# Dense operands on multiples of 512 bytes, early state-space inputs, and seven PSUM banks for the dense products of a two-block model

## The chip, the core and the metric

The kernel runs on one core of one Trainium2 chip. The metric is the device time of one execution in microseconds, less is better. A profile is one execution on the chip, taken by the hardware profiler; its times are counted from the first instruction. Engines are called PE (matrix products), DVE (vector), ACT (activations), POOL (the general engine) and SP (which issues the DMAs).

## The reference, cut to what matters

Two different transformer-like blocks run one after the other on x of 1024 tokens by 1024 channels, all in float32.

```
def reference(x, ...):
    x = first_block(x, ...)     # retention + sparse attention, then conv_ffn
    return second_block(x, ...) # rwkv7 time mix + S5 state space, then gated ffn

first_block:  proj = rmsnorm(x) @ w_in             # 1024 x 6424
              merged = sig(ga) * (retention @ w_ret_o) + sig(gb) * (nsa @ w_nsa_o)
              x = x + merged @ w_out
              x = x + (gelu(conv3(h @ w_up_a)) * (h @ w_up_b)) @ w_down   # 2816 wide
second_block: proj = modulate(rms_norm(x)) @ w_in  # 1024 x 2304
              mix = [rwkv7(z), s5_mix(u)] @ w_out ; x = x + g_m * mix
              x = x + g_f * ((silu(h @ gate) * (h @ up)) @ down)          # 2816 wide
```

`s5_mix` first turns its parameters (`s5_a_re`, `s5_a_im`, `s5_log_dt`, `s5_b`, `s5_c`) into tables: decay and rotation of each state, their powers, and products with b and c. The tables depend on the parameters alone.

## The kernel before, in words

**Dense products.** Activations lie transposed, channels on the 128 partitions and tokens along the row. One dense product (`proj`, with `mm3`, L204) takes 128 output channels by 512 tokens. Each weight block of 128 by 128 and each activation is split into a rounded high part and the rest (`whi`, `wlo`; for instance `fh`, `fl`), and three fp32r matmuls per block are summed: high by high, high by rest, rest by high. A product over 1024 channels is 24 matmuls; one of `ffn`'s down products over 5 or 4 blocks is 15 or 12. Every matmul streams 512 columns (2048 bytes per partition, the moving operand) past 128 columns of weights (512 bytes per partition). `mm3t` (L212) has it the other way round: activations are the stationary operand, and 256 columns of weights (`w2hi`, `w2lo`) are streamed; it is run for the retention's values (768 matmuls) and for `u_proj` (384).

**Weights.** `wload` (L180 to L183): SP loads 512 KB into `wraw` (two buffers, a third one in part of the kernel), ACT rounds it to `whi`, POOL subtracts to get `wlo`. `whi` and `wlo` have two buffers each.

**PSUM.** There are 8 banks of 128 by 512. `PM` (name `mm`) has 2, and every dense product takes one of them in turn; `PN` has 1. The other 5 are given to the stage that runs: in the second part the pools `mb0`, `mb1`, `mb2` of the class `Banks` with 2, 2 and 1 (`b`), which the two chains of the RWKV recurrence, its side work, and (through `any`) transposes and state-space work use. A bank is free again when ACT or DVE has copied its sum out: for the first half of an up product ACT copies to `at` (L1548), for the second DVE multiplies `ct` by it (L1572).

**Order.** Instructions are written in program order, and a scheduler that simulates the engines puts them into each engine's queue; queues run in order. The attention and the RWKV recurrence are small dependent steps. Dense products of other parts (`fill`) are placed between their steps by hand-written dependencies (`beside_attention`, `side_by_side`). The stages, in us: norm and projections to 170, attention with dense products beside it to 640, retention to 940, merge and output of block one to 1170, ffn of block one for the first 512 tokens with the state-space tables (`s5_prep`) step by step beside it to 1600, projections of block two to 1756, state space and recurrence for either half with dense products beside them to 3053, the rest dense to the end.

**State-space tables.** `s5_prep` (L954) is a generator; its first step loads `s5_a` to `s_araw` (L966, L967) and `s5_log_dt` to `s_dt` with two DMAs of 1024 elements of 4 bytes (L976), transposes (L971), takes an exponential on ACT (L977) and runs some 55 small DVE instructions; its second step loads `s_B` (L1048). One step is written after each step of the ffn (`f10`), the first after the ffn's first.

**Addresses.** Tiles are put one after the other, pools stacked from both ends of a partition. Bytes past a multiple of 512 at which a row of an operand begins in the kernel before:

```
whi, wlo (all of wload but the state space's)     160
fh, fl (ffn, half a sequence), yr, yn (merge)     160
ah, al (ffn, hidden)                               96
hh, hl (block one's input), Mh, Ml, mo, mh, ml    480
zh and its own whi, wlo (state space)             480
w2hi, w2lo of the retention / of u_proj       0 / 480
```

All of them are multiples of 32. By the loops, 5,136 of the matmuls of L204 stream an operand at 160 (fh and fl, with wlo: 4,560; yr 384; yn 192), 2,112 one at 96, and 3,120 one at 480.

Of the kernel before, what the change touches and what calls it, by code (L numbers as in the profile page):

```python
# [85 lines left out]


CHUNK_DECAY = [float(np.exp(np.log1p(-np.exp2(np.float32(-5.0 - h))) * np.float32(128.0))) for h in range(4)]


class Banks:
# [12 lines left out]
    def any(self):  # L104
        self.n += 1
        return self.chain((0, 1, 0, 1, 2)[self.n % 5])


class Ctx:
    def __init__(self, tc, I, ctx):  # L110
        self.tc, self.nc, self.I, self.ctx = tc, tc.nc, I, ctx
        self.C = ctx.enter_context(self.pool("C", 1))
        self.PM = ctx.enter_context(self.pool("PM", 2, space=PSUM))
        self.PN = ctx.enter_context(self.pool("PN", 1, space=PSUM))
        self.DR = ctx.enter_context(self.pool("DR", 1, space=DRAM))
        self.ident = self.const("ident", self.C)
        self.ones = self.const("ones", self.C)
        self.W = None
        self.n_ins = 0
        self.WX = None  # L120
        self.n_w = 0

    def pool(self, name, bufs=1, side=None, space=None):
# [7 lines left out]
    def alloc(self, name, bufs=1, side=None):  # L131
        kw = {} if side is None else {"side": side}
        return self.tc.alloc_tile_pool(name=name, bufs=bufs, reuse_waits="tile", **kw)

    def const(self, name, pool):
# [79 lines left out]
    def proj(self, srcs, a, evac, kt=KT, nt=2, pool=None):  # L215
        w = self.wload(srcs, kt, pool)
        for t in range(nt):
            ps = self.PM.tile([128, 512], F32, name="mm")
            self.mm3(ps, w, a, t, kt)
            evac(t, ps)  # L220
# [142 lines left out]
class Nsa:  # L363
    def __init__(self, g, a, w_in, par, dst, dv, cx):
        self.g, self.a, self.w_in, self.par, self.dst, self.dv = g, a, w_in, par, dst, dv
        cp = cx.enter_context(g.pool("nc", 1))
        self.gate = cp.tile([128, 8, 24], F32, name="gate")
        self.kcd = [cp.tile([128, 2, 64], F32R, name=f"kcd{x}") for x in range(2)]
        self.vc4 = cp.tile([128, 2, 128], F32R, name="vc4")
        self.ap = cx.enter_context(g.pool("ac", 1))  # L370
        self.pq = cx.enter_context(g.pool("pq", 2, space=PSUM))
        self.pt = cx.enter_context(g.pool("pt", 2, space=PSUM))
        self.po = cx.enter_context(g.pool("po", 1, space=PSUM))
        self.tsel, self.tedge, self.tcmp = (g.const(n, self.ap) for n in ("tsel", "tedge", "tcmp"))
        self.valid, self.keep, self.force, self.nsl = (g.const(n, self.ap) for n in ("valid", "keep", "force", "nslope"))

# [46 lines left out]
    def compress(self, tp):  # L423

        g, nc, I, par = self.g, self.g.nc, self.g.I, self.par
        for kv, nm in ((0, "k"), (1, "v")):
            w1 = tp.tile([128, 16, 256], F32, name="cw1")
            w2 = tp.tile([128, 2, 64], F32, name="cw2")
            nc.sync.dma_start(w1, I["cmp_w1_" + nm][0].rearrange("(l p) n -> p l n", p=128))
# [8 lines left out]
            for j in range(2):  # L438
# [3 lines left out]
                nc.scalar.activation(hid[:, j], ps, AF.Gelu_apprx_tanh, bias=b1[:, j:j + 1], scale=1.0)  # L442
            c32 = tp.tile([64, 2, 64], F32, name="c32")
            nc.vector.memset(c32, 0.0)
# [273 lines left out]

def retention(g, a, w_in, gn_g, D_, yp, side_job, rest, early):


    with ExitStack() as cx:
        P = {n: cx.enter_context(g.pool("r" + n)) for n in ("tp", "vp")}
        P.update({n: cx.enter_context(g.pool("r" + n, b, space=PSUM)) for n, b in (("p1", 2), ("p2", 2), ("p3", 1))})
        sp = cx.enter_context(g.pool("rsj"))
        P.update({n: g.const(n, P["tp"]) for n in ("zeta", "xi")})
        for h in range(4):
            retention_head(g, a, w_in, gn_g, D_["gab"], D_["yr"], h, P, early)
            if h == 0:
                yn = load_split(g, yp, D_["yn"], 4, "yn")  # L730
            if h == 1:
                r = side_job(sp)
        rest()
    return r, yn
# [160 lines left out]
def nsa_phase(g, par, D_):  # L895
# [16 lines left out]
    with ExitStack() as cx:  # L912
        N = Nsa(g, a, w_in, par, D_["yn"], D_["nv"], cx)
        with g.pool("cp") as cp:
# [3 lines left out]
            N.compress(cp)  # L918
        N.tp = cx.enter_context(g.pool("at", 2))
        for gr in range(2):  # L920
            if gr:
# [31 lines left out]

def s5_prep(g, I, T, bank):  # L954

    nc, tc = g.nc, g.tc
    V, P = nc.vector, nc.gpsimd
    with ExitStack() as cx:
# [5 lines left out]

        are_im = tp.tile([32, 128], F32, name="s_araw")
        nc.sync.dma_start(are_im[0:16], I["s5_a_re_2"][0].rearrange("(a b) p -> a (b p)", b=2))  # L966
        nc.sync.dma_start(are_im[16:32], I["s5_a_im_2"][0].rearrange("(a b) p -> a (b p)", b=2))  # L967
        ps = bank()
# [4 lines left out]
        dt = small("dt")  # L973
        ld = I["s5_log_dt_2"]
        for b in range(2):
            nc.sync.dma_start(dt[b * 64:(b + 1) * 64], bass.AP(tensor=ld.tensor, offset=ld.offset + b, ap=[[0, 64], [2, 16]]))  # L976
        nc.scalar.activation(dt, dt, AF.Exp)  # L977
        x, mag, ang, n, r = (small(k) for k in ("x", "mag", "ang", "n", "r"))
# [529 lines left out]
class Ffn:  # L1508


    def __init__(self, g, D_, par):
        self.g, self.D, self.par = g, D_, par
        self.P = P = g.alloc("F")
        self.h = tuple([P.tile([128, 512], F32R, name=f"f{x}{k}") for k in range(KT)] for x in "hl")
        self.x = [P.tile([128, 512], F32, name=f"fx{k}") for k in range(KT)]
        self.carry = P.tile([128, NF, 2], F32, name="carry")
        self.r = {}
# [40 lines left out]
    def up(self, kind, hf, f, j, last):  # L1558
# [5 lines left out]
        else:  # L1564
            c = P.tile([128, 512], F32, name="ct", bufs=2)
            g.proj(I["ffn_w_gate_2"][0][:, f * 128:(f + 1) * 128], self.h, lambda t, ps: nc.scalar.activation(c, ps, AF.Silu), nt=1)
            w = I["ffn_w_up_2"][0][:, f * 128:(f + 1) * 128]
        hi = P.tile([128, 512], F32R, name=f"ah{j}")
        lo = P.tile([128, 512], F32R, name=f"al{j}")

# [103 lines left out]
class Mixer:  # L1674


    def __init__(self, g, D_, F, par, ad, banks):
        self.g, self.D, self.F, self.par, self.ad, self.banks = g, D_, F, par, ad, banks
        self.zc = F.P.tile([128, 14], F32, name="zc")
        self.s5c = F.P.tile([128, 2, 16], F32, name="s5c")  # L1680
        self.Sc = F.P.tile([128, 4, 2, 64], F32, name="Sc")

# [77 lines left out]
def second_part(g, D_, par, par2, ad, merged, dst):  # L1760
# [19 lines left out]
    def out2(hf):  # L1780
        acc = F.acc("nacc2")
        M.out(hf, acc)
        F.rstd_of(acc, (2, hf))

    acc = F.acc()
    take(out1(g, D_, m, 0, acc, F.P, banks.any, F.x))
# [8 lines left out]
    f10 = F.steps(1, 0)  # L1795
    prep = s5_prep(g, g.I, T, banks.any)
    for _ in range(54):
# [13 lines left out]
    M.z_proj(0, a, x3)  # L1811
    hp.release()
    M.mix(0, U, T)
    up.release()
# [19 lines left out]
    with g.pool("yo", side="right") as F.yo:  # L1834
# [3 lines left out]
        fill = g.products()  # L1838
        side_by_side(g.tc, M.groups, fill, PER_GROUP[1], LAG, SLACK, more=MORE[1])
        out2(1)  # L1840
        F.norm(2, 1)
# [6 lines left out]
    cx.close()  # L1848
    F.P.release()


# [36 lines left out]
def build(tc, I, dst):  # L1888
    with ExitStack() as ctx:
        g = Ctx(tc, I, ctx)  # L1890
        par, par2 = {}, {}
        D_ = {n: g.DR.tile([r, S], F32, name="d_" + n) for n, r in
              (("yn", 512), ("gab", 3 * D + 256 * EARLY), ("yr", D), ("x1", D), ("x3", D), ("x4", D), ("zd", 1792), ("mix", D))}
# [8 lines left out]
        g.W.release()  # L1902
        g.st.release()


# [26 lines left out]
```

## Time and profile before

| | us |
|---|---|
| median of 3 runs | 3532.59 (3530.93 to 3536.27) |
| profiled execution, its own time | 3534.38 |
| its span, first to last instruction | 3532.60 |
| PE busy | 3365.9 (95%) |
| DVE, ACT, POOL busy | 1717.1, 1333.5, 1456.5 |

Read it so: a matmul's record is longer than the time until the next matmul starts, because they are pipelined. Where matmuls follow each other without a gap, the time of one is the distance of starts, and the busy time of PE is their number by that distance. An idle time is told in brackets with what ended it.

### The profile page before, as it was taken

Reading aid. Unit: us, or ns where it says so; the run is one execution under the profiler, and the core shown is the slowest. Engines: PE = TensorE matmul, PEld = TensorE weight load, DVE = VectorE, ACT = ScalarE, POOL = GpSimd, SP = SyncE. Lnnn points to the kernel's source line nnn. Section 1 sums busy time; section 2 is a strip of 40 time slices with the busy share of each in tenths; the row PEclk is TensorE's granted clock in tenths of the full one; section 3 lists DMA queues with packets and bytes.
Section 4 is the critical chain, followed back from the end, with each engine's and each line's share of the span. In section 5 each row is a group of like instructions: output and inputs, shape, how many; then the busy total and the mean of one; then the engine's idle time right before and its main releaser. Section 6 shows DMA issues by size and latency. Waiting matters only on the chain. (4 is left out here: it accounts for less than half of the span.)

```text
span 3532.6 us, 49520 instructions
## 1 busy us (share of the span) xinstructions
PE 3365.9 (95%) x19080; PEld 2721.0 (77%) x19080; DVE 1717.1 (49%) x3317; ACT 1333.5 (38%) x2171; POOL 1456.5 (41%) x1089
## 2 busy tenths in 40 slices
PE   7999999999999798998989999999899999999998
PEld 6988788878788677877877777768777777778887
DVE  4456556465434665345575545565744344341112
ACT  4245346422333322343234434433353433342223
POOL 2333433210144344553555444324554443345544
PEclk9999999999999899999999999989999999999999
DMA  5211111455634334234533122134441222353332
GB/s 147 73 53 52 59 62 43 133 175 167 196 122 137 106 101 149 85 111 120 181 117 115 58 80 67 52 106 150 144 135 58 71 65 61 100 181 96 91 94 90
DMA packets 521845, 371.02 MB, mean 105 GB/s; under 512 B 33756, under 2 KB 457866, under 8 KB 520842
## 3 DMA queue, kind: packets, MB, share of 16 engines
q1 hardware_dynamic: 521610, 367.85, 34.2%
q8 instruction: 151, 2.47, 0.3%
q14 instruction: 84, 0.69, 0.1%
HBM read 313.43 MB, written 54.03 MB: 104 GB/s over the span
## 5 line engine op out<-in xcount | busy, mean ns | idle before, releaser
L183 POOL TENSOR_TENSOR wlo<-wraw,whi 128x1024 fp32r<-128x1024 f32 (+2 forms) x460 | 945.0, 2057 | 1301.7 <-PE mm L204 726.2
L182 ACT ACTIVATE whi<-wraw 128x1024 fp32r<-128x1024 f32 (+2 forms) x460 | 418.1, 909 | 762.0 <-PE mm L204 619.8
L204 PE MATMUL mm<-fh,whi 128*128 128x512 f32 x1520 | 621.2, 410 | 35.3 <-DVE ct L1572 17.8
L204 PE MATMUL mm<-fl,whi 128*128 128x512 f32 x1520 | 610.8, 403 | 6.1 <-DVE fl L308 5.9
L204 PE MATMUL mm<-fh,wlo 128*128 128x512 f32 x1520 | 402.7, 397 | 0.0
L204 PEld LDWEIGHTS mm<-fh,whi 128*128 128x128 f32 x1520 | 292.1, 193 | 107.2 <-DVE ct L1572 16.3
L204 PEld LDWEIGHTS mm<-fl,whi 128*128 128x128 f32 x1520 | 291.6, 192 | 70.1 <-DVE fl L308 10.0
L204 PEld LDWEIGHTS mm<-fh,wlo 128*128 128x128 f32 x1520 | 279.5, 188 | 60.3 <-issue 2.6
L204 PE MATMUL mm<-ah,whi 128*128 128x512 f32 x704 | 283.6, 406 | 10.7 <-DVE ct L1572 7.6
L204 PE MATMUL mm<-al,whi 128*128 128x512 f32 x704 | 282.5, 401 | 0.0
L204 PE MATMUL mm<-hh,whi 128*128 128x512 f32 x640 | 263.3, 412 | 6.9 <-DVE kc L232 3.7
L204 PE MATMUL mm<-hl,whi 128*128 128x512 f32 x640 | 262.8, 411 | 0.0
L204 PE MATMUL mm<-ah,wlo 128*128 128x512 f32 x704 | 201.0, 401 | 0.0
L1572 DVE TENSOR_TENSOR ct<-ct,mm 128x512 f32<-128x512 f32 x88 | 60.1, 684 | 266.1 <-PE mm L204 257.7
L204 PE MATMUL mm<-hh,wlo 128*128 128x512 f32 x640 | 181.8, 405 | 0.0
L204 PEld LDWEIGHTS mm<-ah,whi 128*128 128x128 f32 x704 | 132.4, 188 | 45.5 <-issue 11.0
L204 PEld LDWEIGHTS mm<-al,whi 128*128 128x128 f32 x704 | 132.7, 188 | 30.4 <-issue 1.7
L204 PEld LDWEIGHTS mm<-ah,wlo 128*128 128x128 f32 x704 | 129.0, 188 | 30.0 <-issue 0.3
L204 PEld LDWEIGHTS mm<-hh,whi 128*128 128x128 f32 x640 | 124.0, 194 | 30.3 <-issue 5.6
L204 PEld LDWEIGHTS mm<-hl,whi 128*128 128x128 f32 x640 | 123.5, 193 | 22.0
L204 PEld LDWEIGHTS mm<-hh,wlo 128*128 128x128 f32 x640 | 118.2, 191 | 22.6 <-issue 0.4
L560 ACT ACTIVATE s<-s,amn 128x640 f32<-128x640 f32 (+7 forms) x128 | 94.0, 735 | 79.4 <-DVE amn L556 71.7
(561 smaller groups left out, 6166.3 us busy)
## 6 DMA issues: line engine op xcount, KB each, us to landing
wraw<-in_w_up SPq DMA_DIRECT2D x88, 512.0 KB
wraw<-in_w_in SPq DMA_DIRECT2D x84, 512.0 KB
ada_w<-in_w_ada SPq DMA_DIRECT2D x96, 256.0 KB
wraw<-in_ffn_w_gate SPq DMA_DIRECT2D x44, 512.0 KB
wraw<-in_ffn_w_up SPq DMA_DIRECT2D x44, 512.0 KB
wraw<-in_w_out SPq DMA_DIRECT2D x32, 512.0 KB
d_gab<-st SPq DMA_DIRECT2D x56, 256.0 KB
wraw<-in_w_down SPq DMA_DIRECT2D x48, 256.0 KB
```

Of the source, the lines that this page charges most:

```text
L182: nc.scalar.activation(hi[:, :kt], raw[:, :kt], AF.Copy)
L183: nc.gpsimd.tensor_sub(lo[:, :kt], raw[:, :kt], hi[:, :kt].bitcast(F32))
L204: self.nc.tensor.matmul(ps, w[x][:, k], a[y][k][:, t * 512:(t + 1) * 512], start=i == 0, stop=i == 3 * kt - 1)
L560: nc.scalar.activation(sb[r][:, :n], sb[r][:, :n], AF.Exp, bias=init, scale=-1.0, accum_out=st[:, 0, r:r + 1])
L1572: nc.vector.tensor_tensor(c, c, ps, op=OP.mult)
```

## The change

1. Addresses. A tile of 480 bytes at the top end, padding at the end of the pools `C` and `nc` (`fill`), small tiles moved behind or into other tiles (`valid`, `nslope`, the carries, `w2` and `c32` of the compression, which now use the `st` buffers), pools swapped (`vp` before `tp`) or split (`FA` for `ah`, `al`), and tiles reserved at the start of pools. After it `whi`, `wlo`, `fh`, `fl`, `ah`, `al`, `hh`, `hl`, `yr`, `yn`, `M`, `mo`, `mh`, `ml`, `zh`, `w2hi`, `w2lo` all begin at a multiple of 512.
2. State-space inputs. `s5_raw` loads `s5_a` and `s5_log_dt` at the start of the second part, into one of the two `at` buffers; `s5_log_dt` comes as one DMA of 128 rows of 128 bytes. The first step of `s5_prep` is written ahead of the ffn's first step.
3. PSUM. `Banks.dense` gives each dense product of `proj` one of 7 banks in turn, PM's two and the five of `Banks`, while `g.more` is set: from the start of the second part to the first state-space mix, and from the last output product on. In between, and in block one, there are PM's two as before.

```
+LINE = 512
+FIRST = 16512
+TOP = 480
...
+    def dense(self, first):
+        self.k = getattr(self, "k", 0) + 1
+        i = (None, 0, 1, None, 0, 1, 2)[self.k % 7]
+        return first() if i is None else self.chain(i)
...
+    def fill(self, pool, at=0):
+        n = -(at + pool.current_size() // 128) % LINE
+        if n:
+            pool.tile([128, n // 4], F32, name="pad")
...
     def proj(self, srcs, a, evac, kt=KT, nt=2, pool=None):
         w = self.wload(srcs, kt, pool)
+        pm = lambda: self.PM.tile([128, 512], F32, name="mm")
         for t in range(nt):
-            ps = self.PM.tile([128, 512], F32, name="mm")
+            ps = self.more.dense(pm) if self.more else pm()
...
-            w2 = tp.tile([128, 2, 64], F32, name="cw2")
+            w2 = g.st.tile([128, 512], F32, name="st")[:, :128].rearrange("p (j n) -> p j n", j=2)
...
-        P = {n: cx.enter_context(g.pool("r" + n)) for n in ("tp", "vp")}
+        P = {n: cx.enter_context(g.pool("r" + n)) for n in ("vp", "tp")}
...
+        for n, b in (("pct", 1), ("pth", 2), ("ptl", 2)):
+            N.tp.tile([128, 512], F32R, name=n, bufs=b)
...
+def s5_raw(g, pool):
+    t = pool.tile([128, 514], F32, name="at", bufs=2)
+    I = g.I
+    g.nc.sync.dma_start(t[0:16, 0:128], I["s5_a_re_2"][0].rearrange("(a b) p -> a (b p)", b=2))
+    g.nc.sync.dma_start(t[16:32, 0:128], I["s5_a_im_2"][0].rearrange("(a b) p -> a (b p)", b=2))
+    ld = I["s5_log_dt_2"]
+    g.nc.sync.dma_start(t[:, 128:160], bass.AP(tensor=ld.tensor, offset=ld.offset, ap=[[0, 128], [1, 32]]))
+    return t[0:32, 0:128], t[:, 128:160].rearrange("p (a b) -> p b a", b=2)
...
         for b in range(2):
-            nc.sync.dma_start(dt[b * 64:(b + 1) * 64], bass.AP(tensor=ld.tensor, offset=ld.offset + b, ap=[[0, 64], [2, 16]]))
-        nc.scalar.activation(dt, dt, AF.Exp)
+            r = slice(b * 64, (b + 1) * 64)
+            nc.scalar.activation(dt[r], ldt[r, b], AF.Exp)
...
+        self.A = g.alloc("FA")
...
+    g.more = banks
+    raw = s5_raw(g, F.P)
     acc = F.acc()
     take(out1(g, D_, m, 0, acc, F.P, banks.any, F.x))
...
-    prep = s5_prep(g, g.I, T, banks.any)
+    prep = s5_prep(g, g.I, T, banks.any, raw)
+    take(prep, 1)
     for _ in range(54):
         take(f10, 1)
         take(prep, 1)
...
+    g.more = None
     M.mix(0, U, T)
...
         side_by_side(g.tc, M.groups, fill, PER_GROUP[1], LAG, SLACK, more=MORE[1])
+        g.more = banks
         out2(1)
...
+        top = g.alloc("top", side="right")
+        top.tile([128, TOP // 4], F32, name="pad")
...
+        g.fill(g.C, FIRST)
```

## Rows read from the trace of the kernel before

**Rows 1.** The page: PE's busy time, share, instructions.

```profile
PE 3365.9 (95%) x19080; PEld 2721.0 (77%) x19080; DVE 1717.1 (49%) x3317; ACT 1333.5 (38%) x2171; POOL 1456.5 (41%) x1089
```

**Rows 2.** Busy time by stretch: span, engines (instructions), clock, DMA.

```profile
170.00:640.00 470.00, 463.09 (x2424) 383.11 (x2423) 285.12 (x804) 239.32 (x491) 180.89 (x202) 1.00 0.18 55
1170.00:1330.00 160.00, 137.31 (x689) 111.04 (x688) 104.83 (x283) 46.04 (x66) 67.99 (x44) 0.93 0.37 103
1890.00:2435.00 545.00, 522.97 (x3757) 392.37 (x3756) 296.43 (x585) 220.72 (x366) 225.88 (x176) 0.97 0.29 87
3166.00:3533.00 367.00, 355.48 (x1573) 291.04 (x1571) 57.43 (x81) 106.27 (x139) 183.93 (x106) 0.99 0.32 94
```

**Rows 3.** The same view, matmuls of L204 alone: whole span, then three stretches.

```profile
0.00:3533.00 3533.00, 2613.54 (x10368) 0.98 0.35 105
...
1890.00:2435.00 545.00, 378.30 (x1373) 0.97 0.29 87
2605.00:3053.00 448.00, 319.45 (x1155) 1.00 0.26 76
170.00:640.00 470.00, 305.77 (x1106) 1.00 0.18 55
```

**Rows 4.** Timeline of PE: two fh products' first matmuls, 24 matmuls apart.

```profile
3242.00 0.39 PE L204 MATMUL mm<-fh,whi 128*128 128x512 f32 x1
...
3247.44 0.39 PE L204 MATMUL mm<-fh,whi 128*128 128x512 f32 x1
```

**Rows 5.** Timeline of PE: two ah products' first matmuls, 15 matmuls apart.

```profile
3222.54 0.39 PE L204 MATMUL mm<-ah,whi 128*128 128x512 f32 x1
...
3226.04 0.39 PE L204 MATMUL mm<-ah,whi 128*128 128x512 f32 x1
```

**Rows 6.** Timeline of PE: hh and hl, 14 matmuls from first to last start.

```profile
718.31 0.39 PE L204 MATMUL mm<-hh,whi 128*128 128x512 f32 x1
...
721.52 0.39 PE L204 MATMUL mm<-hh,whi 128*128 128x512 f32 x1
```

**Rows 7.** Timeline of PE: L212 in the retention, 256 columns, runs of 8.

```profile
662.01 1.10 PE L212 MATMUL mm<-w2lo,hh 128*128 128x256 f32 x8
662.94 1.10 PE L212 MATMUL mm<-w2hi,hh 128*128 128x256 f32 x8
```

**Rows 8.** Busy time of PE after the longest stall: span, PE, granted clock.

```profile
1195.00:1200.00 5.00, 5.00 (x13) 0.50 0.52 156
```

**Rows 9.** Timeline of PE there; 8 matmuls from first to last start.

```profile
1193.18 1.86 PE L251 MATMUL pn<-c_ones,nacc 128*128 128x1 f32 x8 [14.59 <-DVE nacc L243]
...
1195.91 0.63 PE L204 MATMUL mm<-fh,whi 128*128 128x512 f32 x1
...
1199.32 0.63 PE L204 MATMUL mm<-fh,whi 128*128 128x512 f32 x1
```

**Rows 10.** Waits of PE from 1071 to 1756 us: total, times, longest.

```profile
PE mm L204 <- DVE ct L1572: 19.1, 6, 5.4
PE pn L251 <- DVE nacc L243: 14.6, 1, 14.6
PE mm L204 <- ACT at L1548: 7.3, 1, 7.3
```

**Rows 11.** Timeline of ACT around that stall.

```profile
1167.77 0.59 ACT L803 COPY st<-b 128x512 f32<-128x512 f32 x1 [1.16 <-PE b L162]
1187.71 1.28 ACT L977 ACT_TABLE_LOAD   x1 [19.35 <-DMA s_dt<-in_s_log_dt]
```

**Rows 12.** Timeline of SP's queue there: start, time to issue.

```profile
1165.90 1.46 SPq L976 DMA_DIRECT2D s_dt<-in_s_log_dt  x2
1167.46 4.12 SPq L1048 DMA_DIRECT2D s_B<-in_s_b_re  x1
1171.62 15.88 SPq L1048 DMA_DIRECT2D s_B<-in_s_b_im  x1
1187.60 1.20 SPq L180 DMA_DIRECT2D wraw<-in_w_up  x1
```

More of the change, by code (lines that the diff above doesn't have):

```diff
@@ L121, in __init__ @@
         self.n_w = 0
+        self.more = None
     def pool(self, name, bufs=1, side=None, space=None):
@@ L366, in __init__ @@
         cp = cx.enter_context(g.pool("nc", 1))
-        self.gate = cp.tile([128, 8, 24], F32, name="gate")
         self.kcd = [cp.tile([128, 2, 64], F32R, name=f"kcd{x}") for x in range(2)]
         self.vc4 = cp.tile([128, 2, 128], F32R, name="vc4")
+        self.gate = cp.tile([128, 8, 24], F32, name="gate")
+        self.valid, self.nsl = (g.const(n, cp) for n in ("valid", "nslope"))
+        g.fill(cp)
         self.ap = cx.enter_context(g.pool("ac", 1))
@@ L374, in __init__ @@
         self.tsel, self.tedge, self.tcmp = (g.const(n, self.ap) for n in ("tsel", "tedge", "tcmp"))
-        self.valid, self.keep, self.force, self.nsl = (g.const(n, self.ap) for n in ("valid", "keep", "force", "nslope"))
+        self.keep, self.force = (g.const(n, self.ap) for n in ("keep", "force"))
     def cmp_proj(self, tp):
@@ L442, in compress @@
                 nc.scalar.activation(hid[:, j], ps, AF.Gelu_apprx_tanh, bias=b1[:, j:j + 1], scale=1.0)
-            c32 = tp.tile([64, 2, 64], F32, name="c32")
+            c32 = g.st.tile([128, 512], F32, name="st")[:64, :128].rearrange("p (j n) -> p j n", j=2)
             nc.vector.memset(c32, 0.0)
@@ L951, in s5_tables, with s5_prep @@
             (("K", 2048), ("bin", 4096), ("car", 2048), ("cai", 2048), ("ec", 2064), ("es", 2064), ("rho", 2064))}
-def s5_prep(g, I, T, bank):
+def s5_raw(g, pool):
[6 more added lines that the diff above has]
+    return t[0:32, 0:128], t[:, 128:160].rearrange("p (a b) -> p b a", b=2)
+def s5_prep(g, I, T, bank, raw):
     nc, tc = g.nc, g.tc
@@ L963, in small @@
             return tp.tile([128, 16], F32, name="s_" + n)
-        are_im = tp.tile([32, 128], F32, name="s_araw")
-        nc.sync.dma_start(are_im[0:16], I["s5_a_re_2"][0].rearrange("(a b) p -> a (b p)", b=2))
-        nc.sync.dma_start(are_im[16:32], I["s5_a_im_2"][0].rearrange("(a b) p -> a (b p)", b=2))
+        are_im, ldt = raw
         ps = bank()
@@ L973, in s5_prep @@
         dt = small("dt")
-        ld = I["s5_log_dt_2"]
         for b in range(2):
-            nc.sync.dma_start(dt[b * 64:(b + 1) * 64], bass.AP(tensor=ld.tensor, offset=ld.offset + b, ap=[[0, 64], [2, 16]]))
-        nc.scalar.activation(dt, dt, AF.Exp)
+            r = slice(b * 64, (b + 1) * 64)
+            nc.scalar.activation(dt[r], ldt[r, b], AF.Exp)
         x, mag, ang, n, r = (small(k) for k in ("x", "mag", "ang", "n", "r"))
@@ L1515, in __init__ @@
         self.x = [P.tile([128, 512], F32, name=f"fx{k}") for k in range(KT)]
-        self.carry = P.tile([128, NF, 2], F32, name="carry")
+        small = P.tile([128, 128], F32, name="carry")
+        self.carry = small[:, 0:44].rearrange("p (f c) -> p f c", c=2)
+        self.zc, self.s5c = small[:, 44:58], small[:, 64:96].rearrange("p (a b) -> p a b", a=2)
+        self.Sc = P.tile([128, 4, 2, 64], F32, name="Sc")
+        for n, b in (("nacc", 1), ("nacc2", 1), ("ct", 2)):
+            P.tile([128, 512], F32, name=n, tag=n, bufs=b)
         self.r = {}
@@ L1567, in up @@
             w = I["ffn_w_up_2"][0][:, f * 128:(f + 1) * 128]
-        hi = P.tile([128, 512], F32R, name=f"ah{j}")
-        lo = P.tile([128, 512], F32R, name=f"al{j}")
+        hi = self.A.tile([128, 512], F32R, name=f"ah{j}")
+        lo = self.A.tile([128, 512], F32R, name=f"al{j}")
         def ev(t, ps):
@@ L1678, in __init__ @@
         self.g, self.D, self.F, self.par, self.ad, self.banks = g, D_, F, par, ad, banks
-        self.zc = F.P.tile([128, 14], F32, name="zc")
-        self.s5c = F.P.tile([128, 2, 16], F32, name="s5c")
-        self.Sc = F.P.tile([128, 4, 2, 64], F32, name="Sc")
+        self.zc, self.s5c, self.Sc = F.zc, F.s5c, F.Sc
     def u_proj(self, a, U, beside, between=lambda: None):
@@ L1849, in second_part @@
     F.P.release()
+    F.A.release()
 def ada(g, par, I, tp):
@@ L1903, in build @@
         g.st.release()
+        top.release()
+        g.fill(g.C, FIRST)
 _INS = ['x', 'norm_mix', 'w_in', 'ret_gn_g', 'cmp_pos_k', 'cmp_w1_k', 'cmp_b1_k', 'cmp_w2_k', 'cmp_pos_v', 'cmp_w1_v',
```

## The prediction

> **What bounds the kernel now.** I read the page's busy times first. PE is busy 95% of the span [rows 1], so only less PE work or fewer PE stalls can shorten it much. Next the busy times by stretch: PE is close to full in the attention, in the recurrence and at the dense end alike [rows 2]; where the tables are made it is not (137 of 160 us). Restricted to the dense matmuls of L204, the same view shows what fills PE: 10,368 matmuls, 2,614 of 3,533 us [rows 3]. So the price of one such matmul is the largest lever here: 1 ns on each is 10.4 us.
>
> That price is read from starts in stretches without gaps. With fh and fl streaming, 24 matmuls take 5.44 us, 226.7 ns each [rows 4]. With ah and al, 15 take 3.50 us, 233.3 ns [rows 5]. With hh and hl, 14 take 3.21 us, 229.3 ns [rows 6]. The three do the same work at the same granted clock with the same weight buffers; what differs is where the operand begins: 160, 96 and 480 bytes past a multiple of 512. [...]
>
> **Part 1, addresses.** No instruction is removed; each dense matmul gets a new price p, which no row shows for both operands at a multiple of 512. [...] From above: 233.3 ns, the worst of the three. [...] The spread of 226.7 to 233.3 at one and the same weight address says that the stream's address does matter. I take p = 217, a small rest above the bound from below, because both operands move; 214 to 221 counts as the same case.
>
> The sum at 217: 5,136 matmuls at 160 save 9.7 each, 49.8 us; 2,112 at 96 save 16.3, 34.4 us; 3,120 at 480 save 12.3, 38.4 us; the 1,152 of L212 with 256 columns go from 116.3 to about 110, 7.3 us. Together 130 us. Not all of it shortens the end: 3,634 of the matmuls stand beside the attention and the recurrence [rows 3], where the order is fixed by hand and the small steps need their time. They would save about 11.5 each, 42 us; PE has 523 of 545 us filled there [rows 2] and hardly waits, so the small steps are nearly always ready, but a faster filler uses up their slack. I take a quarter, 10 us, as lost. Net 120 us. [...]
>
> [...]
>
> **Part 2, state-space inputs.** The longest stall of PE is 14.6 us, for a sum over `nacc` [rows 9, 10]. DVE could not add because ACT had not squared: ACT stood 19.35 us at L977 for `s_dt` [rows 11], whose 2,048 elements of 4 bytes crept in; behind them SP needed 4.1 and 15.9 us to issue the two loads of `s_B`, and the next weight load came after that, at 1187.6 [rows 12]. Behind ACT's wait stood the square, the next `whi` and the copy to `at`. After it PE ran 5 us at half clock, 13 matmuls that lose 0.2 us each [rows 8]: 2.6 us. The change loads these inputs about 100 us before they are used, `s_log_dt` in 128 rows of 128 bytes, so ACT's wait goes: up to 17.2 us. What is late next is the load of `s_B`: 4,096 rows of 64 bytes on SP, ahead of weight loads, unchanged. The two or three weight buffers cover most of its time; I take 3 us as coming back. Net 14 us, between 5 and 17. The moved step itself: three DMAs on SP ahead of output loads (about 1 us each to issue, block one's last products are still running), one small transpose, one exponential more, some 55 small DVE instructions ahead of the ffn's first steps, when DVE has room (105 of 160 us busy). They cost nothing on PE unless DVE is late, and then the banks below cover it. The held `at` buffer is read before the ffn's second tile needs it.
>
> **Part 3, banks.** In the first stretch with seven banks PE waits 19.1 us for L1572 and 7.3 us for the copy to `at` [rows 10], both times because the bank was not emptied: DVE was busy with tables, ACT with a norm. With five more banks PE can go on. It gets not all of it back: ACT still needs a free `at` buffer, DVE a free `ct`, the down products need the last hidden tile, and the 7.3 us lie in a norm whose own chain is long, so PE may idle a little later instead. A new wait comes in: a dense product can get a bank that a table's transpose holds until DVE or ACT empties it, and then PE's whole queue stands behind it. The bounds are 0 and 26.4 us, and 3 more where the clock stays up; I take 18. In the last stretch PE waits little, so nothing there.
>
> Sum: 120 + 14 + 18 = 152 us from 3534.4 us, the profiled execution's own time (its span is 3532.6), gives 3382; the median of the runs shown is 1.8 us below it, so **3380 us**, 4.3% faster. With 214 ns and all stalls gone it would be 3336, with 221 ns 3423.
>
> **Rivals.**
> *Half of it.* Alignment helps, but the two streams still disturb each other, p about 224.5: the classes save 2.2, 8.8 and 4.8 ns, 45 us, with the stalls' 32 us 3457. [...]
> *Only small units count.* If reads go by lines of 16 or 32 bytes, all old addresses were aligned already and p stays; only the stalls go, 32 us: 3502. [...] Against it: three prices at three addresses that are all multiples of 32 [rows 4 to 6].
> *Slower.* Stream and weights now begin at the same offset everywhere; if the two reads meet in the same part of the memory at every line, p could be 233.3 for all. Rows 7 speak for it: per column its aligned stream is as slow as the worst case (0.454 ns against 0.456). The classes at 160 and 480 then lose 34 and 12 us, 46 in all, against 32 from the stalls: 3548. The mean price now is 228.8; 32 us are 3.1 ns on each of 10,368, so it decides from 231.9 ns on. Against it: the class at 160 has both operands at the same offset and is the fastest.
>
> **How the numbers follow.** Chances: forecast (p of 214 to 221) 0.65, half 0.2, only small units 0.08, slower 0.07. The forecast's own range is 3336 to 3423. From 3335 to 3500 the forecast and the half case are held, less a margin for stalls that move elsewhere: 8 in 10. A measurement of this kernel tells a change from none above about 0.2%, 7 us. The first three cases are faster by more than that except for the edge of the third, the fourth is slower by 0.4%: faster 0.91, same 0.03, slower 0.06.
>
> **What would show it.** Part 1: starts of fh, ah and hh matmuls at one common distance of 214 to 221 ns, and 256 columns at about 110; L204's busy time down from 2,614 to about 2,490 us. Part 2: no ACT wait at L977, no PE wait for `nacc`. Part 3: the waits for L1572 and `at` gone before the first state-space mix. The prediction is wrong if the distance stays above 224, if rows of the recurrence show new waits of PE for DVE that eat more than 10 us, or if dense products wait for banks that transposes hold.

## The result and the profile after

The changed kernel takes 3496.61 us (median of 4 runs, 3491.14 to 3502.92), the kernel before 3532.99 beside it: ratio 0.9897, 95% interval 0.9876 to 0.9917. It is 1.0% faster, 36 us where 152 were forecast; the time is inside the range, near its upper end. The profiled execution took 3491.14 us, the least of the four, with a span of 3489.4. One execution of the kernel of experiment 9 below, the profiled one, took 5626.23 us at a granted clock of 0.65 and is left out of its time. Line numbers have moved: L204 is now L221, L212 is L229, L162 is L179, L1644 is L1680, L1572 is L1608.

The page of the kernel after, its busy row, answers to [rows 1]; PE has lost 22.6 us of busy time:

```profile
PE 3343.3 (96%) x19080; PEld 2713.5 (78%) x19080; DVE 1706.9 (49%) x3317; ACT 1338.4 (38%) x2176; POOL 1451.0 (42%) x1089
```

The busy times of the kernel after for the dense matmuls alone, over the whole span (columns as in [rows 3]):

```profile
0.00:3490.00 3490.00, 2593.89 (x10368) 0.98 0.35 106
```

So 19.7 us less than in [rows 3], where the forecast wanted some 120. Some 8 of these are the clock and not the addresses: the dense records at a granted clock of 0.50 went from 68.3 to 50.9 us, and 47% of that time is counted as lost, as worked out below. The timeline of PE in the kernel after says why; the pairs are fh (24 matmuls apart), ah (14), hh (15) and the 256-column matmuls (8):

```profile
3197.83 0.39 PE L221 MATMUL mm<-fh,whi 128*128 128x512 f32 x1
...
3203.27 0.39 PE L221 MATMUL b<-fh,whi 128*128 128x512 f32 x1
...
3174.71 0.39 PE L221 MATMUL b<-ah,whi 128*128 128x512 f32 x1
...
3177.88 2.43 PE L221 MATMUL b<-ah,wlo 128*128 128x512 f32 x10
...
712.22 0.39 PE L221 MATMUL mm<-hh,whi 128*128 128x512 f32 x1
...
715.62 0.39 PE L221 MATMUL mm<-hl,whi 128*128 128x512 f32 x1
...
644.67 1.12 PE L229 MATMUL mm<-w2hi,hl 128*128 128x256 f32 x8
645.63 1.12 PE L229 MATMUL mm<-w2lo,hh 128*128 128x256 f32 x8
```

That is 5.44 us over 24, 3.17 over 14, 3.40 over 15: 226 to 227 ns for all three. The class at 160, half of all dense matmuls, costs what it cost before [rows 4]; ah has come down from 233.3 [rows 5] and hh from 229.3 [rows 6]; the 256-column ones have gone up, from 116.3 [rows 7] to 120.

The stalls did move. Waits of PE in the kernel after from 1152 to 1600 us, that is the stretch with the tables:

```profile
PE b L179 <- DMA s_craw<-in_s_c_im: 5.5, 3, 2.0
PE b L179 <- DVE s_ba L1062: 3.8, 1, 3.8
PE b L221 <- ACT whi L199: 3.3, 1, 3.3
PE mm L229 <- ACT mh L325: 3.3, 2, 2.7
PE b L179 <- DMA s_craw<-in_s_c_re: 1.9, 1, 1.9
```

The three waits of [rows 10], 41 us, are gone, and new ones have come in: a transpose (L179) that waits for its input with the dense products behind it in PE's queue, and weights (`whi`) that ACT has not split yet. And at the end there are these rows, of the kernel before from 3490 us and of the kernel after from 3440 us:

```profile
PE b L162 <- POOL fx L1644: 2.0, 1, 2.0
...
PE b L179 <- POOL fx L1680: 8.5, 4, 2.8
```

By stretches, from the first matmul of each (the retention from the end of the attention's last product), before and after: retention 300.8 and 288.2 us, feed-forward with the tables 472.3 and 436.3, state-space projections behind it 117.2 and 122.3, second half's state-space and recurrence with its output 621.4 and 617.7, last output norm to the end 415.4 and 422.5; the others differ by less than 2.

Where the 43 us between the two spans went can be worked out from the whole traces: the time in which PE has no record, the time of its records at a granted clock of 0.50 (there a 512-column matmul took 426 ns [rows 9] instead of 227 [rows 4], so 47% of it is counted as lost, an estimate from these two), and the rest.

| us | before | after | addresses alone | inputs and addresses |
|---|---|---|---|---|
| span | 3532.6 | 3489.4 | 3506.6 | 3488.1 |
| PE without a record | 166.7 | 146.1 | 158.4 | 147.3 |
| PE's records at half clock | 113.0 | 84.3 | 104.8 | 88.7 |
| rest: span less the first, less 0.47 of the second | 3312.8 | 3303.6 | 3298.9 | 3299.2 |

(The last two columns are experiments below.) From before to after 20.6 us come from idle time, 13.5 from the clock, and only 9 from what full-clock work costs, the term on which the forecast rested. These are two single executions. Executions of one and the same kernel differ in the clock too: the kernel before, beside experiments 3 and 10 to 12, took 3528.69 us at a mean granted clock of 0.981 and 3550.91 us at 0.974. So the clock's share is that of these two executions, which stand 43 us apart where the medians stand 36 apart.

### The profile page after: what moved, and what is told of

Same layout as the page of the kernel before. It is cut to its first block, busy times and chain, and to the rows that moved or that the text cites. A ratio compares the mean times of both kernels' runs of the same rounds, so it can differ in the third digit from the quotient of the medians.

```text
span 3489.4 us, 49450 instructions
## 1 busy us (share of the span) xinstructions
PE 3343.3 (96%) x19080; PEld 2713.5 (78%) x19080; DVE 1706.9 (49%) x3317; ACT 1338.4 (38%) x2176; POOL 1451.0 (42%) x1089
## 5 line engine op out<-in xcount | busy, mean ns | idle before, releaser
L221 PE MATMUL mm<-fh,whi 128*128 128x512 f32 x976 | 398.1, 410 | 6.5 <-ACT fh L325 3.9
L221 PE MATMUL mm<-fl,whi 128*128 128x512 f32 x976 | 390.4, 401 | 7.8 <-DVE fl L326 7.7
L221 PE MATMUL mm<-fh,wlo 128*128 128x512 f32 x976 | 271.6, 405 | 0.0
L221 PE MATMUL mm<-hh,whi 128*128 128x512 f32 x640 | 261.3, 409 | 5.4 <-DVE kc L250 3.7
L221 PE MATMUL mm<-hl,whi 128*128 128x512 f32 x640 | 261.8, 409 | 0.0
L221 PEld LDWEIGHTS mm<-fh,whi 128*128 128x128 f32 x976 | 183.8, 189 | 52.4 <-issue 5.2
L221 PEld LDWEIGHTS mm<-fl,whi 128*128 128x128 f32 x976 | 183.8, 189 | 49.5 <-DVE fl L326 12.3
L221 PE MATMUL b<-fh,whi 128*128 128x512 f32 x544 | 214.1, 394 | 3.3 <-ACT whi L199 3.3
L221 PE MATMUL b<-fl,whi 128*128 128x512 f32 x544 | 213.2, 392 | 0.0
L221 PEld LDWEIGHTS mm<-fh,wlo 128*128 128x128 f32 x976 | 179.1, 190 | 40.7 <-issue 4.1
L221 PE MATMUL mm<-ah,whi 128*128 128x512 f32 x438 | 178.7, 410 | 6.9 <-DVE ct L1608 6.3
L221 PE MATMUL mm<-hh,wlo 128*128 128x512 f32 x640 | 178.1, 400 | 0.0
L221 PE MATMUL mm<-al,whi 128*128 128x512 f32 x438 | 175.9, 402 | 0.0
L221 PEld LDWEIGHTS mm<-hh,whi 128*128 128x128 f32 x640 | 122.7, 192 | 28.1 <-issue 5.5
L221 PEld LDWEIGHTS mm<-hl,whi 128*128 128x128 f32 x640 | 122.9, 192 | 21.1
L221 PE MATMUL b<-fh,wlo 128*128 128x512 f32 x544 | 135.8, 392 | 1.8 <-POOL wlo L200 1.8
L221 PEld LDWEIGHTS mm<-hh,wlo 128*128 128x128 f32 x640 | 117.0, 189 | 21.6
L221 PE MATMUL mm<-ah,wlo 128*128 128x512 f32 x438 | 127.0, 403 | 0.0
L221 PEld LDWEIGHTS b<-fh,whi 128*128 128x128 f32 x544 | 103.2, 190 | 25.5 <-ACT whi L199 4.0
```

The source lines that it names most:

```text
L221: self.nc.tensor.matmul(ps, w[x][:, k], a[y][k][:, t * 512:(t + 1) * 512], start=i == 0, stop=i == 3 * kt - 1)
```

## Experiments

Each ratio is to the kernel before, run beside it on the same chip (medians 3536.7, 3536.1 and 3535.9 us). Edits are shown in part, against the kernel that the text names, or against the kernel after where it names none.

**1. Is 226.7 ns the floor, and what in an address sets the price?** A kernel with nothing but matmuls, 16 (`RUN`) for each pair of start offsets: m bytes past a multiple of 512 for the streamed operand, w for the stationary one, in steps (`STEP`) of 32:

```diff
+        def run(m, w, n=512, cols=128, run=RUN, same=False):
...
+            for i in range(run):
+                j = i % 8
+                ws = W[:, (0 if same else j * 128) + w // 4:][:, :cols]
+                nc.tensor.matmul(ps[:cols, :n], ws, M[:, j * 512 + m // 4:][:, :n], start=i == 0, stop=i == run - 1)
...
+        for w in range(0, 512, STEP):
+            for m in range(0, 512, STEP):
+                run(m, w)
```

> Computes none of the reference: 4,000-odd fp32r matmuls back to back, 16 for each pair of start offsets (streamed operand and stationary operand at 0, 32, ... 480 bytes past a multiple of 512), then other widths, fewer stationary columns, one stationary operand used 16 times, and bf16, all at offset 0 or 256. Theory 'a fixed price': 226.7 ns for 512 columns at (0, 0) and about 120 ns for 256, so some 13 ns are paid per matmul whatever its width when both operands are aligned; offsets change it by up to about 7 ns more. No pair of offsets is below 225 ns. With one and the same stationary operand the price stays at 226.7 if the fixed part belongs to the matmul, and falls towards 213 if it belongs to the load of weights. Rival 'aligned at the same place is a collision': some pair with the two operands at different offsets is near 213 to 218 ns, (0, 0) is not the cheapest.

Its timeline, the runs of 16 for w = 0 and m = 0, 32, 64, 96 and 128 bytes; the distance of two rows by 16 is the price:

```profile
26.70 3.79 PE L45 MATMUL pb<-mv,wt 128*128 128x512 f32 x16
30.32 3.90 PE L45 MATMUL pa<-mv,wt 128*128 128x512 f32 x16
34.06 3.83 PE L45 MATMUL pb<-mv,wt 128*128 128x512 f32 x16
37.73 3.89 PE L45 MATMUL pa<-mv,wt 128*128 128x512 f32 x16
41.46 3.89 PE L45 MATMUL pb<-mv,wt 128*128 128x512 f32 x16
...
984.42 2.96 PE L45 MATMUL pb<-mv,wt 128*128 128x384 f32 x16
987.22 2.93 PE L45 MATMUL pa<-mv,wt 128*128 128x384 f32 x16
...
1012.10 3.63 PE L53 MATMUL pb<-mb,wb 128*128 128x512 bf16 x16
1015.56 1.91 PE L53 MATMUL pa<-mb,wb 128*128 128x256 bf16 x16
```

The first four distances give 226, 234, 229 and 233 ns. Over the 256 pairs of this run the price went by m - w modulo 256. In steps of 32 from 0 it is 227, 233.6, 229.4, 233.1, 233.2, 234.1, 232.7, 232.7 ns, each within 2 ns wherever the pair begins. No pair is below 226.6: the theory holds in that, and its rival, that equal offsets collide, is the reverse of what was measured for 512 columns. Fewer columns at offsets of 0 modulo 256 cost 173 to 175 (384) and 119 to 120 (256). From 256 to 512 that is 107 ns for 256 columns more, 0.42 ns per column, and by estimate some 13 ns on top (226.7 less twice 107). 128 columns don't fit this: they cost 108 to 112, where 0.42 ns a column and 13 on top would make some 66. bf16 costs 216.5 for 512 columns. The three classes of before have their places in this table: fh and its weights, 160 and 160, differ by 0 (227); hh, 480 and 160, by 64 (229.4); ah, 96 and 160, by 192 (232.7). What was "at 160" was aligned already, to its partner. Why the distance counts, no run here shows.

**2. Other widths, small steps, half clock.** The same kernel with other runs, some behind a stop of PE of 16 us:

```diff
+        for n in (512, 384, 280, 256):
+            for m in range(0, 512, 32):
+                run(m, 0, n)
+        for m in range(4, 68, 4):
+            run(m, 0)
...
+        for m in (0, 32, 64, 160, 0, 32):
+            for _ in range(4):
+                nc.scalar.activation(M2, raw, AF.Copy)
+            run(m, 0, mv=M2)
```

> Computes none of the reference: runs of 16 fp32r matmuls as in the first sweep, now with the streamed operand at 0, 32, ... 480 and the stationary one at 0 for 512, 384, 280 and 256 columns, then steps of 4 bytes of either operand for 512 columns, one bank against two by turns, one operand repeated, bf16, and runs of 16 that follow a stop of some 15 us, for the half clock. Theory 'the difference of the two offsets sets it': for 512 columns 227 at differences 0 and 256 and 229 to 234 elsewhere; for 256 columns another difference than 0 is cheaper, near 116 at 480, since the kernel before had 116.3 there and the changed one has 120; bf16 shows no dependence; at half clock all offsets cost 426. Rival 'columns plus 32 cycles': 256 columns are 120 at every difference, and the 116.3 has another cause. Rival 'the bank is the price': with two banks by turns 512 columns fall towards 213.

Timeline of the 256-column runs, m from 160 to 224 and 256 to 288 bytes, w = 0:

```profile
172.96 2.04 PE L57 MATMUL pb<-mv,wt 128*128 128x256 f32 x16
174.83 1.99 PE L57 MATMUL pa<-mv,wt 128*128 128x256 f32 x16
176.66 2.05 PE L57 MATMUL pb<-mv,wt 128*128 128x256 f32 x16
178.55 2.08 PE L57 MATMUL pa<-mv,wt 128*128 128x256 f32 x16
180.47 2.05 PE L57 MATMUL pb<-mv,wt 128*128 128x256 f32 x16
```

For 256 columns 192 bytes apart is cheapest, 114.4 ns (174.83 to 176.66); 256, which is 0, costs 120 (178.55 to 180.47); at 32, where the kernel before stood in the retention, it is 118 (the kernel had 116.3 [rows 7]; the 2 ns between are not explained). So alignment took the narrow class to one of its dearest places. 384 columns cost 173.2 to 176.4, with 0 neither the cheapest nor the dearest. Offsets that are no multiples of 32 bytes cost 229.6 to 239.6 for 512 columns. Two banks by turns, a repeated operand or repeated weights leave 227 to 228. bf16 costs 215.8 to 216.5 at every offset tried of its streamed operand. Behind the stops, 16.4 us each in the trace, PE ran for a time at a granted clock of 0.50 (rows of the busy times: span, PE, PEld, ..., granted clock; offsets of 160 and of 32):

```profile
474.00:477.00 3.00, 3.00 (x9) 2.32 (x8) 0.00 (x0) 0.00 (x0) 0.00 (x0) 0.50 0.00 0
518.00:522.00 4.00, 4.00 (x11) 3.14 (x10) 0.00 (x0) 0.00 (x0) 0.00 (x0) 0.50 0.00 0
```

There starts are 426 to 427 ns apart at offsets of 0, 32, 64 and 160 alike, where full clock has 227 to 234 for the same offsets. So the price at half clock didn't tell what could be had at full clock.

**3. Does the difference of offsets set the price in the kernel too?** Base is the kernel of experiment 5; the weight buffers move by 96 bytes, and padding makes up for it, so that the other operands keep their places modulo 256:

```diff
-TOP = 480
+TOP = 224
...
-        n = -(at + pool.current_size() // 128) % LINE
+        n = ((96 if at else 0) - at - pool.current_size() // 128) % LINE
...
         lo = W.tile([128, m, 128], F32R, name="wlo", bufs=nb)
+        if pool is None:
+            W.tile([128, 40], F32, name="wpad", bufs=1)
```

> The kernel of the early state-space inputs without seven banks (3491.65 us), with the weight buffers moved by 96 bytes, so that in 10,272 of the 512-column matmuls the two operands begin 160 bytes apart modulo 256; same instructions in the same order. Theory 'the difference of the two offsets sets the price': 234.1 ns in place of 226.7 by the sweep, 7.4 ns each, 76 us if all of it shows and 50 if a third is covered beside attention and recurrence: 3541 to 3568, slower than before the change (ratio 1.002 to 1.010). Rival 'the price in the kernel has another cause than the sweep's': within 10 us of 3492.

3538.89 us (12 runs), ratio 1.0005 (0.9993 to 1.0018), against 0.9874 for its base: 47 us slower, the whole gain gone with the same instructions. Timeline of PE, two fh products 24 matmuls apart:

```profile
3240.30 0.39 PE L223 MATMUL mm<-fh,whi 128*128 128x512 f32 x1
...
3245.92 0.39 PE L223 MATMUL mm<-fh,whi 128*128 128x512 f32 x1
```

5.62 us, 234.2 ns each, as in the first experiment. Of 76 us 47 show, a little less than the lower expectation; the attention takes 3.3 us more and the first recurrence 6.3, the dense end 13.

**4. The addresses alone.** The early inputs and the seven banks taken back:

```diff
-    g.more = banks
-    raw = s5_raw(g, F.P)
...
-    prep = s5_prep(g, g.I, T, banks.any, raw)
-    take(prep, 1)
+    prep = s5_prep(g, g.I, T, banks.any)
...
-        g.more = banks
```

> The addresses alone; state-space inputs and banks as before. Theory 'price 226.7 for all': 2,112 ah matmuls save 6.6 ns each (13.9 us), 3,120 at 480 save 2.6 (8.1 us), 1,152 of 256 columns lose 3.5 (4 us), the 5,136 at 160 save nothing; 18 us, some of it lost beside the recurrence: 3518 us (3510 to 3524). Rival 'the gain is the stalls': within 5 us of before. Rival 'addresses bring all of it and the other parts cancel': 3497.

3509.28 us, ratio 0.9921 (0.9906 to 0.9936): 28 us, more than the 18 that the prices give. By the table above 14 are price; the other 12 of the profile's 26 are idle time and half clock. Most of those are in the retention, 300.8 to 291.3 us.

**5. The inputs too, without the banks.** `s5_raw` and the first table step are in, `g.more` stays None:

```diff
-    g.more = banks
     raw = s5_raw(g, F.P)
...
-        g.more = banks
```

> Addresses and the early state-space inputs, no dense product over seven banks anywhere. Theory 'each part has its own stall': the inputs alone take the wait for nacc away (14.6 us, and 2 to 3 of half clock), the stretch with the tables is 453 to 457 us against 470 with the addresses alone and 437 with both: 3493 to 3497 on the scale of the earlier runs, where the addresses alone gave 3509. Rival 'DVE is as late anyway': the stall appears again at L1600 and the time is that of the addresses alone, within 4 us.

3491.65 us, 0.9874 (0.9859 to 0.9888): 17 us more than the addresses alone, in the expected place (the stretch with the tables 444.6 us against 470.0). It is as fast as the whole change or faster. Its waits of PE from 1150 us, as in [rows 10], have no `nacc`, and the two others are still there:

```profile
PE mm L221 <- DVE ct L1608: 11.9, 3, 9.8
PE mm L221 <- ACT at L1584: 7.4, 1, 7.4
```

**6. The banks without the inputs.** Experiment 4 with the banks up to the first state-space mix:

```diff
+    g.more = banks
     acc = F.acc()
     take(out1(g, D_, m, 0, acc, F.P, banks.any, F.x))
```

> Addresses and the seven banks up to the first state-space mix (not in the last stretch), with the state-space inputs loaded where they were. Theory 'each part has its own stall': the banks can't cover a wait of the norm's sum, 450 to 456 us in the stretch with the tables and 3500 in all. Rival 'the banks alone would do': dense products go on into other banks while DVE waits, and the time is that of the change without the last stretch's banks, 3488, within 4 us.

3515.64 us, 0.9937 (0.9924 to 0.995): no faster than the addresses alone; neither theory's gain is there. The waits of PE from 1150 us:

```profile
PE pn L269 <- DVE nacc L261: 14.6, 1, 14.6
PE b L221 <- ACT whi L199: 10.7, 2, 5.6
PE b L179 <- DVE s_ba L1054: 7.1, 1, 7.1
```

The 14.6 us of [rows 9] are untouched by banks, as the first theory had it. The stretch with the tables takes 460.1 us against 470.0, and the projections behind it 124.0 against 112.7: what the banks give in the first is taken back in the second.

**7. Everything but the addresses.** The kernel before with the inputs early and the banks.

```diff
+    g.more = banks
+    raw = s5_raw(g, F.P)
...
+        g.more = banks
```

> State-space inputs early and the seven banks, with the addresses as before. Theory: the stretch with the tables loses about 29 of the 36 us that it lost in the full change, the state-space stretches and the last one give back 15 to 20: 3518 us (3510 to 3526), and the two halves add up to the whole. Rival 'the stalls only move': within 5 us of before, and the addresses have the whole 1%.

3525.46 us, 0.9962 (0.9948 to 0.9976): 11 us, at the edge of what was expected, because the last stretch (428.8 against 415.4 us) costs more than I had counted. With experiment 4 it adds up: 28 and 13 us by the ratios, 36 in the whole change.

**8. The change without the last stretch's banks.**

```diff
-        g.more = banks
         out2(1)
         F.norm(2, 1)
```

> The full change, but in the last stretch (the second block's output, its norm, the last feed-forward) dense products use their own two banks alone. Theory 'transposes hold the banks at the end': the last chunk's tail is 38 us again in place of 46.8, the waits of PE for the output's copies fall from 12.6 to about 2 us, 3487 us (8 to 10 less than the full change). Rival 'the end is set by the output's stores whatever PE does': the same as the full change within 3 us.

3487.86 us, 0.9857 (0.9838 to 0.9877), some 9 us better than the whole change. Waits of PE from 3444 us to the end:

```profile
PE b L179 <- POOL fx L1680: 2.0, 1, 2.0
```

The time and the waits are as expected. With seven banks the down products and the output's transposes share banks, and PE's queue stands behind transposes whose `fx` POOL has not finished; with two banks of their own for the dense products three of the four waits are gone (8.5 us in the kernel after, 2.0 here).

**9. The banks only until the feed-forward with the tables is through**, without the projections behind it, on experiment 8.

```diff
+    g.more = None
     M.u_proj(a, U, x3)
     M.z_proj(0, a, x3)
     hp.release()
-    g.more = None
```

> The full change, with the seven banks only up to the end of block one's feed-forward of the first half, neither in the state-space projections after it nor in the last stretch. Theory 'the projections take a transpose's bank too': that stretch goes from 123.4 us back to 113 to 117, 3480. Rival 'the late weights and hidden halves come from the shorter stretch before': it stays at 120 or more, 3486 to 3489.

3492.76 us (three executions), 0.9872 (0.9857 to 0.9887): not better than experiment 8, and above even the rival's 3486 to 3489. The time speaks for the rival, that the projections lose their 10 us to the work ahead of them being done sooner and not to their own banks; the stretch itself is not measured here, so this isn't shown.

**10. The 256-column weights 192 bytes apart**, on the kernel of experiment 5:

```diff
-TOP = 480
+TOP = 224
...
+        pool.tile([128, 48], F32, name="w2pa")
         hi = pool.tile([128, kt, 256], F32R, name="w2hi")
         lo = pool.tile([128, kt, 256], F32R, name="w2lo")
+        pool.tile([128, 16], F32, name="w2pb")
```

> The same kernel (3491.65 us), with the 256-column weight tiles 192 bytes further, so that 1,152 matmuls of 256 columns go from 0 to 192 bytes apart; the sweep has 118.9 and 114.5 ns for these. Theory 'the best difference depends on the width': 4.4 to 5.5 ns less each, 5 to 6 us: 3486. Rival 'these stretches wait for something else' (768 of the 1,152 stand in the retention, where PE has pauses): within 2 us of 3491.65 although the starts are 114 to 115 ns apart.

3488.14 us, 0.986 (0.984 to 0.988), 3.5 us better by the medians, with overlapping intervals. The price is as expected; timeline of PE, two runs of 8 in the retention (0.91 us, 114 ns each, where the kernel after has 120):

```profile
646.55 1.07 PE L231 MATMUL mm<-w2hi,hl 128*128 128x256 f32 x8
647.46 1.07 PE L231 MATMUL mm<-w2lo,hh 128*128 128x256 f32 x8
```

The edit doesn't reach all 1,152: in `u_proj` for the first 512 tokens (192 matmuls) most starts are 118 ns apart.

**11 and 12. The loads of `s_C` early, alone and with experiment 10's edit**, both on experiment 8:

```diff
+        craw = tp.tile([128, 8, 64], F32, name="s_craw")
+        for ri, nm in enumerate(("s5_c_re_2", "s5_c_im_2")):
+            nc.sync.dma_start(craw[:, ri * 4:ri * 4 + 4], I[nm][0].rearrange("(t g) c p -> (g c) t p", g=8))
         BB = tp.tile([128, 3, 16, 16], F32, name="s_BB")
...
-                raw = bp.tile([128, 64], F32, name="s_craw")
-                nc.sync.dma_start(raw, cv[t])
                 ps = bank()
-                g.transpose(ps[0:64, 0:128], raw)
+                g.transpose(ps[0:64, 0:128], craw[:, ri * 4 + t])
```

> The change without the last stretch's banks (3487.86 us), with the eight loads of s_C issued as two, two steps earlier, into a tile of their own. Theory 'the banks' gain is spent in new waits of PE behind transposes': the 7.7 us that PE waits for s_craw go, and 5 to 8 us of them reach the end: 3481. Rival 'PE then waits for the weights split on ACT (whi) instead': within 3 us of 3487.86.

> Both of the last two edits on the change without the last stretch's banks. If both theories hold: 3475 to 3477 us, 1.65% below before. If neither: 3487.

3484.46 us, 0.9853 (0.9831 to 0.9875), and 3484.16, 0.9851 (0.9831 to 0.9871): by the intervals no different from experiment 8. PE's waits for `s_craw` are gone, and the stretch with the tables is 5.8 us shorter (431.4 against 437.2) in experiment 11. But the first recurrence takes 12 us more, 552.2 against 540.2, with the same instructions and the same waits of PE. The busy times of its last 100 us, in experiment 8 and then in experiment 11 (span, PE, PEld, DVE, ACT, POOL, granted clock):

```profile
2297.00:2397.00 100.00, 93.46 (x556) 73.84 (x555) 58.53 (x95) 31.46 (x55) 38.37 (x27) 1.00 0.55 172
```

```profile
2287.00:2398.00 111.00, 105.03 (x588) 82.20 (x588) 63.28 (x100) 31.37 (x55) 41.72 (x29) 0.92 0.52 161
```

The clock was lower there, 0.92 against 1.00, which is 9 us of these 111. Over the whole recurrence PE's records at half clock are 48.0 us against 19.6, which is worth 13. It is no accident of one execution: experiment 12, with the same early loads, takes 552.8 us there, also with 48.0 at half clock. The pauses of PE are the same in all three. In experiments 11 and 12 half clock sets in after five of them, of 2.03, 2.14, 1.27, 1.51 and 1.55 us; in experiment 8 the same five stand there, and it sets in after the third alone. Why isn't shown by any run here and stays open. Experiments 8 and 10 to 12 all beat both kernels; among them no order can be told.

## Why the prediction was wrong

**What failed is the price p.** "I take p = 217" made 130 of the 152 us; measured is 226.7. No run shows the 217, the bound from below that it was put above, or the "about 110" of the sum for 256 columns: in experiment 1 no pair of offsets is below 226.6 for 512 columns, and in experiment 2 256 columns cost 114.4 at best. The three classes saved 0, 6.6 and 2.6 ns, and L212 lost 3.7: 13.9 + 8.1 - 4.3, 18 us in place of 130. (The loss is a little high: it counts all 1,152 of L212, and `u_proj`'s 384 stood at 118 to 120 already.) The dense matmuls' busy time fell by 19.7, with the clock's 8 in it. Two readings led there. The first is the bound from below. It was 213 ns, half of the 426.2 that a matmul took at half clock (8 in 3.41 us [rows 8, 9]), taken as the price at full clock without any delay: the author's estimate. Experiment 2 shows 426 to 427 at half clock at each of the four offsets tried, so the half-clock row had no word on addresses, and at full clock 226.7 was measured at the best of them, 13.6 ns above that half. The second is the word "aligned" itself: I compared addresses with a multiple of 512, where by experiment 1 the price goes by the distance of the two operands modulo 256. The sentence that would have told me stands in the prediction, as an argument against a rival: the class at 160 "has both operands at the same offset and is the fastest". Read as what sets the price and not as a point against something, it gives 226.7 for all and 18 us. That the time still lies inside the stated range is luck: the range was built on prices of 214 to 224.5 ns, none of which came, and the clock, which the sum had only at single stalls (2.6 and 3 us), gave a part of the gain.

**The rivals.** The time came out nearest to "only small units count" (3502), whose mechanism is refuted: the old addresses were all multiples of 32 and cost 226.7 to 233.3, and experiment 3 takes back 47 us by 96 bytes. In the sweep the prices repeat after 256 bytes (227 ns at 0 and at 256). "Slower" has it upside down: equal offsets were the cheapest for 512 columns, 227 ns against 229.4 to 234.1. Its argument from rows 7, that per column the aligned stream is as slow as the worst case, took for a price per column what experiment 1 puts at 0.42 ns per column and some 13 ns on top.

**The quarter lost beside attention and recurrence** was right in kind and too small: the attention got less than 2 us faster of some 460, and in experiment 3 the price rise of 7.4 ns is 18 us on the 2,479 dense matmuls of the attention and the first recurrence [rows 3], of which 9.6 show.

**The state-space inputs** were about right: 14 us forecast, between 5 and 17; 17 measured (experiment 4 to 5), at the upper end, with the waits for `s_dt` and `nacc` gone.

**The banks** were sized wrong, and in the last stretch they cost time where I had put nothing. I took 18 us for the first stretch. The stalls of [rows 10] did go, yet the net is -6 us with the inputs early (0.9874 to 0.9857, intervals overlap) and +6 without them (0.9921 to 0.9937), nothing that can be told from zero. In both pairs the stretch with the tables gets shorter and the projections behind it get as much longer: 444.6 to 437.2 and 112.9 to 123.4 us with the inputs early, 470.0 to 460.1 and 112.7 to 124.0 without. PE comes sooner to transposes whose input is not there (waits for `s_craw`: 7.7 us in experiment 8, 9.8 in experiment 6), and to weights that ACT has not split (waits of products in the five banks for `whi`: 6.1 us in the projections of experiment 8, 10.7 from the tables on in experiment 6). "In the last stretch PE waits little, so nothing there" cost 9 us. The wait that did it is close to the one that I had named for the first stretch: PE's whole queue stands behind a transpose. But by the rows the transpose waits for its input `fx` from POOL; no wait in the rows of the kernel after is a dense product's for a transpose's bank. I had looked for what the banks could cover there, found nothing, and did not ask what they could block.

**What I did not count**, but for those single stalls, is the clock. PE's records at half clock fell from 113 to 84 us, worth 13.5 us, a third of the gain in the profile. Busy times of the retention, in the kernel before and then after:

```profile
637.00:937.00 300.00, 274.55 (x1632) 242.62 (x1633) 161.36 (x306) 78.84 (x127) 43.82 (x18) 0.95 0.53 167
```

```profile
635.00:923.00 288.00, 264.93 (x1634) 234.62 (x1634) 158.50 (x306) 81.82 (x130) 43.31 (x18) 0.99 0.56 176
```

The same matmuls in 12 us less, at 0.99 instead of 0.95, and 0.04 of 300 is 12: this stretch, the second largest gain, is nearly all clock by these rows. Eleven traces agree: the retention's idle time is 20 to 29 us and its rest 262 to 265 in each, and those with 3 to 7 us at half clock take 287 to 291 us, those with 22 to 28 take 301 to 302. What kept the clock up is open, and it isn't the number of pauses alone: the retention has 15 pauses of PE over 0.4 us before, 24.6 us together, and 14 after, 21.3 us, but half clock sets in six times before and once after. No run changed the clock alone.

## What to carry to other kernels

Before moving an operand, work out what the present classes have in common with each other and not only with a round number: here three prices and three address pairs already pointed to it, and a run of bare matmuls gives the whole table at once. A floor read at another clock or in another type was a floor only there: half of the 426 ns at half clock and the 216 of bf16 didn't come for fp32r at full clock (226.7 at best), and the best distance of 512 columns, 0, was not that of 256 columns, 192. When queues get more buffers, ask in every stretch what can now stand in front of what: here shared banks cost some 9 us at the end, where PE had hardly waited before (2.0 us from 3490 us on, 8.5 after the change).

## What the hardware showed

At a granted clock of 1.00 an fp32r matmul of 512 columns cost 227 ns at best and up to 234 by the distance of its operands modulo 256 (steps of 32 bytes; experiments 1 to 3). 256 columns cost 114.4 to 120 with another best place, 192 (experiments 2 and 10). A narrow one of 128 columns cost 108 to 112, about twice the 54 ns that 0.42 ns per column would make (experiment 1). bf16 showed no such dependence on its streamed operand (215.8 to 216.5), and fp32r at half clock none at the four offsets tried (426 to 427; experiment 2). The same instructions with the same waits ran 12 us apart in the recurrence, with 48.0 us of PE's records at half clock against 19.6 (experiments 11 and 8).
